# Buffers, addresses and order at the joints of a two-block transformer kernel: second buffers for normalized tiles and transposed matrices, raw weights in other places, loads and transposes in another order

## The chip, the cores and the metric

The kernel runs on one core of one Trainium2 chip. The metric is the device time of one execution in microseconds (us). The engines are TensorE (PE), VectorE (DVE), ScalarE (ACT), GpSimd (POOL) and SyncE (SP); SP issues nearly all the DMAs here, from one queue in order.

## What is computed

The input is 1024 tokens of width 1024 in fp32. A first block of two layers (attention of four kinds, gated projection, layer norm) gives x. The change concerns the second block:

```python
def swiglu(x, w_gate, w_up, w_down):
    return (jax.nn.silu(x @ w_gate) * (x @ w_up)) @ w_down
...
        h = h + 0.5 * swiglu(rms_norm(h, ffn1_norm[i]), ffn1_w_gate[i], ffn1_w_up[i], ffn1_w_down[i])
        u = rms_norm(h, mix_norm[i])
        z = u @ w_in[i]
        q, k, v, s_in, gates = jnp.split(z, splits, axis=-1)
...
        h = h + (g_attn * y_attn + g_ssm * y_ssm) @ w_out[i]
        h = h + 0.5 * swiglu(rms_norm(h, ffn2_norm[i]), ffn2_w_gate[i], ffn2_w_up[i], ffn2_w_down[i])
        h = h + (p[i] @ ple_w_proj[i]) * jax.nn.sigmoid(rms_norm(h, ple_norm[i]) @ ple_w_gate[i])
    return rms_norm(h, final_norm)
```

Between the two feed-forwards stand neighbourhood attention (y_attn) and a two-directional state-space branch (y_ssm), whose small matrices the kernel forms from the parameters. The feed-forward's hidden width is 2816.

## The kernel before

Every fp32 number that a product takes is split in two parts, hi and lo, and a product is three matmuls: hi by hi, lo by hi, hi by lo (`mm3`, L196 to L198). Splitting is done by ACT (the hi copy) and DVE or POOL (the lo difference); `operand` (L1009, L1010) does it for raw weights, into a ring of whi and wlo. Tokens are worked on as eight tiles of 128, four to a half. The order of instructions on each engine is set by a scheduler that takes the program's order as priority and a time model of its own; the chip runs each engine's list in that order. A new tile at the address of an older one waits for the older one's last use, so pool sizes and the order of allocation decide waits.

**Normalizing a tile.** `rms_tile` squares a tile on ACT (L945, into xn as scratch), takes the inverse root on DVE and POOL (L540, L541), and scales on DVE into xn (L947). PE transposes xn in eight 128x128 pieces, by `halves_in` (L960) ahead of a feed-forward and by `rms_T` (L258) behind one. xn has one buffer.

**Up phase** (`ffn_up`). A product of 2x2 blocks is formed from seven block products, which need sums of blocks of x (s1 to s4) and of the weights (t1 to t4). `halves_in` makes the x sums of tiles 4 to 7 with the single buffers a21, a11, s1, s2; `fourth` (L989, L998) makes the last one for four tiles. Raw weights come as `top` and `bot` [128, 4, 256] (L1061); POOL makes t1 to t4 of them (L1069 to L1072). These tiles lie in a late pool that opens over the tiles of `halves_in`. Eleven pairs of gate and up matrices follow; each finished hidden piece is stored at once (L1083).

**Down phase** (`ffn_down`). For each half of the tokens and each half of the columns there are 22 steps. A step loads a hidden piece (`hraw`, three buffers, L1128; only for the first column half), splits it (L1129, L1130), loads a weight piece (L1132; `draw` in even steps, `wraw` in odd ones, two buffers each) and does 12 matmuls. Beside the first half runs a generator `also`: in the first feed-forward it is `ssm_matrices`, which makes M and C on DVE (`cmul`, L1181 and L1184) for each of two directions, then 32 small products into Gp (L1273), then eight groups of two pairs of transposes (L1281), copied by ACT into gW (one buffer, L1283) and stored (L1285). C is stored in four large pieces (L1269). When a half is finished, `then` normalizes and transposes its tiles, the second half's with a priority put back by 150 (`later`).

```python
            for t in range(4):
                with self.later(hf * 150):
                    then(hf * 4 + t, h[t])
```

In the first block's last layer, the output tiles z (three buffers) go from the layer norm straight to a store (L1657) and to `rms_tile`.

## Time and profile before

| what | value |
|---|---|
| runs | 3683.14, 3685.1, 3699.77 us |
| median | 3685.1 us |
| profiled execution, its own time | 3689.25 us |
| its span, first to last instruction | 3687.4 us |
| PE busy | 3380.2 us (92%) |
| DVE, ACT, POOL busy | 2181.0, 1389.2, 1246.1 us |
| mean granted clock of PE | 0.955 |

The stages of the second block in the span: entry to the first up phase at about 1185 to 1256 us, its steady part to 1655, the first down phase to about 2032, the input products of the mix behind it; entry to the second up phase at 2826 to 2886, the second down phase from 3295 to 3542, and the last products to the end. PE is busy nearly all the time, so the time lost is the idle time of PE and the time in which its granted clock is at the lower of its two levels (1.2 instead of 2.4 GHz, shown as 0.50). Both are read by stretch.

### The profile page before, as it was taken

Reading aid. Unit: us, or ns where it says so; the run is one execution under the profiler, and the core shown is the slowest. Engines: PE = TensorE matmul, PEld = TensorE weight load, DVE = VectorE, ACT = ScalarE, POOL = GpSimd, SP = SyncE. Lnnn points to the kernel's source line nnn. Section 1 sums busy time; section 2 is a strip of 40 time slices with the busy share of each in tenths; the row PEclk is TensorE's granted clock in tenths of the full one; section 3 lists DMA queues with packets and bytes.
Section 4 is the critical chain, followed back from the end, with each engine's and each line's share of the span. In section 5 each row is a group of like instructions: output and inputs, shape, how many; then the busy total and the mean of one; then the engine's idle time right before and its main releaser. Section 6 shows DMA issues by size and latency. Waiting matters only on the chain. (4 is left out here: it accounts for less than half of the span.)

```text
span 3687.4 us, 53510 instructions
## 1 busy us (share of the span) xinstructions
PE 3380.2 (92%) x18872; PEld 2935.1 (80%) x18872; DVE 2181.0 (59%) x4926; ACT 1389.2 (38%) x3029; POOL 1246.1 (34%) x1082
## 2 busy tenths in 40 slices
PE   8999899999999599997869899798999799989988
PEld 7999798888888488876648688677789688878878
DVE  5656666656668766669241149435875866652235
ACT  3446645445646332323222131235632332333322
POOL 4232224333223633324314223162322533324522
PEclk9999999999999799997969899899999899999999
DMA  6667863567862222215443453467644322235433
GB/s 222 173 204 215 257 208 101 177 195 212 258 216 94 94 81 89 80 58 176 149 130 121 112 185 115 121 203 218 193 160 135 109 75 85 82 136 190 151 130 115
DMA packets 475355, 555.32 MB, mean 151 GB/s; under 512 B 45248, under 2 KB 318016, under 8 KB 475088
## 3 DMA queue, kind: packets, MB, share of 16 engines
q1 hardware_dynamic: 465872, 541.42, 47.4%
q10 hardware_dynamic: 9216, 10.49, 0.9%
q8 instruction: 150, 2.46, 0.3%
q14 instruction: 117, 0.96, 0.1%
HBM read 398.68 MB, written 153.06 MB: 150 GB/s over the span
## 5 line engine op out<-in xcount | busy, mean ns | idle before, releaser
L186 POOL TENSOR_SCALAR whi<-wraw 128x512 fp32r<-128x512 f32 (+1 forms) x288 | 185.6, 654 | 939.5 <-PE G L197 391.7
L196 PE MATMUL G<-xh,whi 128*128 128x512 f32 x1180 | 469.1, 398 | 3.4 <-DVE slo L161 2.6
L198 PE MATMUL G<-xh,wlo 128*128 128x512 f32 x1180 | 464.1, 394 | 0.0
L196 PE MATMUL G<-whi,xh 128*128 128x256 f32 (+2 forms) x1472 | 438.4, 298 | 27.7 <-ACT whi L1009 17.6
L197 PE MATMUL G<-wlo,xh 128*128 128x256 f32 (+2 forms) x1472 | 431.1, 293 | 0.0
L197 PE MATMUL G<-xl,whi 128*128 128x512 f32 x1064 | 420.4, 395 | 0.2 <-DVE xl L158 0.2
L196 PEld LDWEIGHTS G<-whi,xh 128*128 128x128 f32 x1472 | 282.5, 192 | 35.0 <-ACT whi L1009 18.5
L197 PEld LDWEIGHTS G<-wlo,xh 128*128 128x128 f32 x1472 | 282.4, 192 | 3.6
L188 POOL TENSOR_TENSOR wlo<-wraw,whi 128x512 fp32r<-128x512 f32 (+1 forms) x208 | 266.2, 1294 | 4.8
L196 PEld LDWEIGHTS G<-xh,whi 128*128 128x128 f32 x1180 | 223.7, 190 | 51.0 <-DVE slo L161 2.8
L198 PEld LDWEIGHTS G<-xh,wlo 128*128 128x128 f32 x1180 | 223.4, 189 | 45.7
L198 PE MATMUL G<-whi,xl 128*128 128x256 f32 (+2 forms) x832 | 249.6, 300 | 0.0
L198 PE MATMUL G<-whi,xh 128*128 128x256 f32 (+1 forms) x832 | 243.8, 294 | 0.6 <-DVE xh L1130 0.6
L197 PEld LDWEIGHTS G<-xl,whi 128*128 128x128 f32 x1064 | 201.9, 190 | 39.4 <-DVE xl L158 0.5
L1009 ACT ACTIVATE whi<-t 128x512 fp32r<-128x512 f32 x176 | 105.9, 624 | 320.2 <-PE G L197 147.1
L1010 POOL TENSOR_TENSOR wlo<-draw,whi 128x512 fp32r<-128x512 f32 x88 | 117.2, 1332 | 244.4 <-ACT whi L1009 241.4
L158 DVE TENSOR_TENSOR ptl<-T,pth 128x512 fp32r<-128x512 f32 (+2 forms) x296 | 181.7, 629 | 20.2 <-ACT pth L157 17.0
L502 PE MATMUL T<-ident,P 128*128 128x128 f32 x1064 | 185.4, 278 | 6.7 <-DVE P L481 5.7
L157 ACT ACTIVATE pth<-T 128x512 fp32r<-128x512 f32 (+2 forms) x296 | 156.3, 553 | 55.0 <-PE T L502 51.5
L509 PE MATMUL O<-pth,hv 128*128 128x256 f32 (+1 forms) x616 | 165.3, 280 | 9.4 <-ACT pth L157 3.1
L1071 POOL TENSOR_TENSOR t<-bot,top 128x512 f32<-128x512 f32 x44 | 65.6, 1492 | 316.6 <-DVE wlo L1010 314.9
L509 PE MATMUL O<-ptl,hv 128*128 128x256 f32 (+1 forms) x616 | 162.4, 295 | 5.4 <-DVE ptl L158 4.7
(570 smaller groups left out, 9200.2 us busy)
## 6 DMA issues: line engine op xcount, KB each, us to landing
wraw<-w_in SPq DMA_DIRECT2D x144, 256.0 KB, 3.3
wraw<-ffn_w_down SPq DMA_DIRECT2D x88, 256.0 KB, 3.0
hid<-r SPq DMA_DIRECT2D x88, 256.0 KB, 2.0
hraw<-hid SPq DMA_DIRECT2D x88, 256.0 KB, 3.7
draw<-ffn_w_down SPq DMA_DIRECT2D x88, 256.0 KB, 2.9
wraw<-w_out SPq DMA_DIRECT2D x64, 256.0 KB, 3.5
hk<-ka SPq DMA_DIRECT2D x48, 256.0 KB, 4.8
top<-ffn_w_gate SPq DMA_DIRECT2D x22, 512.0 KB, 3.7
```

What stands on the lines that cost most here:

```text
L157: nc.scalar.activation(hi, ps, AF.Copy)
L158: nc.vector.tensor_tensor(lo, ps, f(hi), op=OP.subtract)
L186: self.nc.gpsimd.tensor_scalar(hi, raw, 1.0, 0.0, op0=OP.mult, op1=OP.add)
L188: eng.tensor_tensor(lo, raw, f(hi), op=OP.subtract)
L196: t.matmul(out, lh, rh, start=first and i == 0, stop=False)
L197: t.matmul(out, lh, rl, start=False, stop=False)
L198: t.matmul(out, ll, rh, start=False, stop=last and i == n - 1)
L502: nc.tensor.transpose(ps[:, c + i * 128:c + i * 128 + 128], rows[bi][j], self.ident)
L509: nc.tensor.matmul(O[:, o:o + n], vs[j], p[:, c:c + n], start=nmm == 0, stop=not units and gi == len(grp) - 1 and x == 1, skip_group_check ...
L1009: self.nc.scalar.activation(as_src(hi), src, AF.Copy)
L1010: lo_eng.tensor_tensor(as_src(lo), src, as_src(f(hi)), op=OP.subtract)
L1071: nc.gpsimd.tensor_tensor(t3, b22, b12, op=OP.subtract)
```

## The change

The diff's core, in the order of the program:

```diff
 def rms_T, Next.done, second feed-forward's loop
-        x = self.T(p, [128, 1024], F32, "xn", 1)
+        x = self.T(p, [128, 1024], F32, "xn", 2)
 Next.tile
-                return K.T(p, [128, 1024], F32, "z", 3)
+                return K.T(p, [128, 1024], F32, "z", 2)
 def ffn_up
         p = late()
+        for n in ("t1", "t2", "t3", "t4"):
+            self.T(p, [128, 4, 128], F32, n, 1)
+        for n in ("th", "r3", "r4"):
+            tile(p, n, 2)
+        stores = []
+        def store():
+            for o, k, c in stores:
+                nc.sync.dma_start(hid[o:o + 128, k:k + 512], c)
+            stores.clear()
...
-                        o = j * 256 + n * 128
-                        nc.sync.dma_start(hid[o:o + 128, hf * 512:hf * 512 + 512], c)
+                        stores.append((j * 256 + n * 128, hf * 512, c))
                 done(c11, 0, 0)
+                if i == 0:
+                    store()
...
+        store()
 def ffn_down(..., delay=0)
                     if c == 0:
-                        raw = self.T(p, [128, 512], F32, "hraw", 3)
-                        nc.sync.dma_start(raw, hid[k * 128:k * 128 + 128, hf * 512:hf * 512 + 512])
-                        nc.scalar.activation(hi, raw, AF.Copy)
-                        nc.vector.tensor_tensor(lo, raw, f(hi), op=OP.subtract)
-                    raw = self.T(*((self.wp, [128, 512], F32, "wraw") if k % 2 else (p, [128, 512], F32, "draw")), 2)
+                        for i in range(3) if k == 0 else [k + 2] if k < 20 else []:
+                            raw = self.T(p, [128, 512], F32, "hraw", 3)
+                            nc.sync.dma_start(raw, hid[i * 128:i * 128 + 128, hf * 512:hf * 512 + 512])
+                            nc.scalar.activation(H[i][0], raw, AF.Copy)
+                            nc.vector.tensor_tensor(H[i][1], raw, f(H[i][0]), op=OP.subtract)
+                    raw = self.T(p, [128, 512], F32, "draw", 1) if k % 3 == 0 else self.T(self.wp, [128, 512], F32, "wraw", 2)
...
-                with self.later(hf * 150):
+                with self.later(hf * delay):
 calls of ffn_down: delay 60 in the first feed-forward, 400 in the second
 def ssm_matrices
+            def group(gp):
                 ps = self.PS("O", self.nO)
-                W = self.T(p, [128, 2, 2, 2, 64], F32, "gW", 1)
+                W = self.T(p, [128, 2, 2, 2, 64], F32, "gW", 2)
...
             for k in range(1, 9):
                 self.cmul(C[...])
-                if k % 2 == 0:
-                    yield
+                yield
+                if k == 2:
+                    (the 32 products into Gp, and Gs)
+                elif k > 2:
+                    group((k - 3) * 2)
             (the four stores of C)
-            (the 32 products into Gp, and Gs; the eight groups, a yield after every second)
+            for gp in (12, 14):
+                yield
+                group(gp)
 second feed-forward's set-up
         p = self.pool("xn2", 1)
+        g = self.rms_gain(p, I["ffn2_norm_2"])
+        for n in ("a21", "a11", "s1", "s2"):
+            self.T(p, [128, 4, 128], F32, n, 1)
+        for _ in range(2):
+            self.T(p, [128, 1024], F32, "xn", 2)
         h.append(p.tile([128, 4, 1024], F32, name="h1"))
-        g = self.rms_gain(p, I["ffn2_norm_2"])
```

In words: normalized tiles get two buffers and z two instead of three. In the late pool t1 to t4 and the small result tiles come first, so `top` and `bot` lie at other addresses: `top` over the layer norm's gains and `bot` over z, where they had lain over the norm's gain rg and over a21 and a11. The program lists the hidden stores one matrix later. The down phase lists its hidden loads up to three steps ahead and has three raw weight buffers instead of four. The second half's normalizing has its priority put back by 60 or 400 instead of 150. In `ssm_matrices` the small products and the transposes' groups are listed between the steps of C, and gW has two buffers. Lines behind about L1050 move by 10 to 22.

Three places show what the engines' lists make of this. On ACT, at the entry to the first up phase (T_16313 and T_16398 are the transposes of tiles 5 and 6; a their first copies; the xn of z_16380 and z_16465 belong to tiles 6 and 7), the list was before

```order
L975 ACTIVATE a_3833_16323<-T_16313 128x512
L945 ACTIVATE xn_16391,rms_16392<-z_16380 128x1024
L157 ACTIVATE xh_3806_16217<-T_16318 128x4x128
L157 ACTIVATE xl_3807_16218<-s_3835_16325 128x4x128
L157 ACTIVATE sb_16219<-s_3836_16333 128x4x128
L157 ACTIVATE sc_16220<-a_3833_16323 128x4x128
L975 ACTIVATE a_3851_16408<-T_16398 128x512
L945 ACTIVATE xn_16474,rms_16475<-z_16465 128x1024
```

and is now

```order
L157 ACTIVATE sc_16220<-a_3815_16238 128x4x128
L1009 ACTIVATE whi_16428<-wraw_16447 128x512
L945 ACTIVATE xn_16391,rms_16392<-z_16380 128x1024
L1038 ACTIVATE r_3837_16340<-G_16347 128x512
L975 ACTIVATE a_3833_16323<-T_16313 128x512
L945 ACTIVATE xn_16474,rms_16475<-z_16465 128x1024
L157 ACTIVATE xh_3806_16217<-T_16318 128x4x128
```

The squares of tiles 6 and 7 have each moved one tile forward: tile 7's stand behind the copy of tile 5, not of tile 6.

On PE, at the end of the first half's products of the first down phase (eh, el the last hidden pieces; gen, xl the second direction's parameters and matrices), the list was before

```order
L198 MATMUL S_20467<-whi_21033,el_19620 128x512
L1281 MATMUL O_20418<-ident,xl_4472_19884 128x128 x2
L1281 MATMUL O_20427<-ident,xl_4472_19884 128x128 x4
L1273 MATMUL O_20839<-gen_19831,xl_4556_20527 128x32 x32
L1281 MATMUL O_20873<-ident,xl_4556_20527 128x128 x4
```

and is now

```order
L198 MATMUL S_20443<-whi_20979,el_19627 128x512
L1282 MATMUL O_20552<-ident,xl_4481_19899 128x128 x4
L1295 MATMUL O_20806<-gen_19846,xl_4568_20584 128x32 x32
L1282 MATMUL O_20881<-ident,xl_4568_20584 128x128 x4
L1282 MATMUL O_20912<-ident,xl_4568_20584 128x128 x4
```

One pair of the first direction's transposes less stands behind the products (a row of four is a group of two pairs); the second direction's 32 small products and all its eight groups still stand behind them.

On PE, in the input products behind the first down phase (T the transposes of xn; G the products), the list was before

```order
L198 MATMUL G_22276<-xh_4616_21098,wlo_22189 128x512
L258 MATMUL T_22091<-ident,xn_22084 128x128 x4
L258 MATMUL T_22098<-ident,xn_22084 128x128 x4
L258 MATMUL T_22112<-ident,xn_22105 128x128 x4
L258 MATMUL T_22119<-ident,xn_22105 128x128 x4
L258 MATMUL T_22133<-ident,xn_22126 128x128 x4
L258 MATMUL T_22140<-ident,xn_22126 128x128 x4
L196 MATMUL G_22302<-xh_4765_22061,whi_22158 128x512
```

and is now, for the last tile,

```order
L198 MATMUL G_22283<-xh_4623_21105,wlo_22196 128x512
L258 MATMUL T_22140<-ident,xn_22133 128x128 x4
L258 MATMUL T_22147<-ident,xn_22133 128x128 x4
L196 MATMUL G_22309<-xh_4772_22068,whi_22165 128x512
```

The transposes of tiles 5 to 7 stood together behind the first half's products; now only tile 7's do, and those of tiles 4, 5 and 6 stand among the products, with 24, 24 and 17 matmuls to the next.

## Rows read from the trace of the kernel before

**Rows 1.** Windows: busy us (instructions) of PE, PEld, DVE, ACT, POOL; PEclk; DMA share; GB/s.

```profile
1200.00:1250.00 50.00, 15.25 (x71) 12.30 (x69) 35.19 (x40) 17.39 (x30) 29.75 (x23) 0.65 0.10 32
...
1350.00:1400.00 50.00, 50.00 (x223) 41.39 (x222) 33.78 (x48) 15.80 (x28) 14.18 (x10) 1.00 0.31 95
...
1850.00:1900.00 50.00, 23.66 (x92) 17.16 (x91) 18.21 (x46) 7.28 (x19) 0.00 (x0) 0.50 0.29 84
...
2050.00:2100.00 50.00, 41.99 (x180) 34.50 (x179) 9.33 (x16) 9.97 (x19) 16.70 (x19) 0.86 0.27 85
...
3550.00:3600.00 50.00, 37.29 (x282) 35.98 (x280) 25.40 (x46) 16.58 (x46) 8.56 (x13) 0.83 0.41 149
```

**Rows 2.** Timeline of PE, 1216 to 1256: start, length, line, [idle before <-releaser].

```profile
1216.40 1.94 PE L960 MATMUL T<-ident,xn 128*128 128x128 f32 x8 [5.03 <-DVE xn L947]
...
1225.27 1.94 PE L960 MATMUL T<-ident,xn 128*128 128x128 f32 x8 [6.93 <-DVE xn L947]
...
1255.39 0.80 PE L196 MATMUL S<-sb,whi 128*128 128x512 f32 x1 [28.18 <-ACT whi L1009]
```

**Rows 3.** Timeline of ACT, tile 6's and tile 7's first copies, tile 6's last.

```profile
1217.52 0.60 ACT L975 ACTIVATE a<-T 128x512 f32<-128x512 f32 x1 [3.96 <-PE T L960]
...
1221.81 0.63 ACT L157 ACTIVATE sc<-a 128x512 fp32r<-128x512 f32 x1 [0.59 <-POOL a L983]
...
1226.39 0.60 ACT L975 ACTIVATE a<-T 128x512 f32<-128x512 f32 x1 [3.96 <-PE T L960]
```

**Rows 4.** Timelines of POOL (three rows) and DVE (two), the same entry.

```profile
1220.51 1.27 POOL L983 TENSOR_TENSOR a<-a,a 128x512 f32<-128x512 f32 x1
...
1222.70 1.34 POOL L989 TENSOR_TENSOR a<-xh,sa 128x512 f32<-128x512 f32 x1
...
1253.41 1.26 POOL L1070 TENSOR_TENSOR t<-bot,t 128x512 f32<-128x512 f32 x1 [5.89 <-DMA bot<-ffn_w_gate]
...
1191.95 1.28 DVE L947 SCALAR_TENSOR_TENSOR xn<-z,rrs,rg 128x1024 f32<-128x1024 f32 x1
...
1222.85 2.28 DVE L947 SCALAR_TENSOR_TENSOR xn<-z,rrs,rg 128x1024 f32<-128x1024 f32 x1
```

**Rows 5.** Timeline of PE, state-space matrices of the second direction, 1829 to 1901.

```profile
1829.38 0.52 PE L1281 MATMUL O<-ident,xl 128*128 128x128 f32 x2 [2.63 <-ACT gW L1283]
...
1848.07 0.61 PE L1273 MATMUL O<-gen,xl 128*128 128x32 f32 x2 [18.17 <-DVE xl L1181]
...
1863.35 0.69 PE L1281 MATMUL O<-ident,xl 128*128 128x128 f32 x2 [0.69 <-ACT gen L1275]
...
1883.75 0.69 PE L1281 MATMUL O<-ident,xl 128*128 128x128 f32 x2 [8.63 <-ACT gW L1283]
...
1888.55 0.69 PE L1281 MATMUL O<-ident,xl 128*128 128x128 f32 x2 [0.47 <-ACT gW L1283]
...
1891.07 0.69 PE L1281 MATMUL O<-ident,xl 128*128 128x128 f32 x2 [1.83 <-ACT gW L1283]
...
1900.03 0.80 PE L196 MATMUL G<-whi,xl 128*128 128x512 f32 x1 [0.99 <-ACT xl L1129]
```

**Rows 6.** Timeline of PE, transposes of finished tiles (L258).

```profile
1929.39 1.94 PE L258 MATMUL T<-ident,xn 128*128 128x128 f32 x8 [3.01 <-DVE xn L947]
...
2059.86 1.94 PE L258 MATMUL T<-ident,xn 128*128 128x128 f32 x8 [4.06 <-DVE xn L947]
...
3554.56 1.73 PE L258 MATMUL T<-ident,xn 128*128 128x128 f32 x7 [4.00 <-DVE xn L947]
```

**Rows 7.** Timeline of PE, entry to the second up phase.

```profile
2867.16 1.97 PE L960 MATMUL T<-ident,xn 128*128 128x128 f32 x8 [6.46 <-DVE xn L947]
```

**Rows 8.** Timeline of PE, first direction's small products (L1273).

```profile
1731.54 0.63 PE L1273 MATMUL O<-gen,xl 128*128 128x32 f32 x2 [11.64 <-DVE xl L1181]
```

**Rows 9.** The page's DMA issues (KB each, median us to landing); timeline of SP.

```profile
draw<-ffn_w_down SPq DMA_DIRECT2D x88, 256.0 KB, 2.9
...
3289.84 0.90 SPq L1128 DMA_DIRECT2D hraw<-hid  x2
```

More of the change, by code (lines that the diff above doesn't have):

```diff
@@ L1104, in four, with ffn_down @@
         return [(W[0][:, k * 128:k * 128 + 128], W[1][:, k * 128:k * 128 + 128]) for k in range(4)]
-    def ffn_down(self, hid, wd, src, dst, p, slots, then, also=None):
+    def ffn_down(self, hid, wd, src, dst, p, slots, then, also=None, delay=0):
         nc = self.nc
@@ L1285, in ssm_matrices @@
                 nc.sync.dma_start(self.win_d[:, b0:b0 + 4, :], W.rearrange("p q e x s -> p (q e) (x s)"))
-                if gp % 4 == 2:
-                    yield
+            for k in range(1, 9):
+                src = (cc[:, 0], cc[:, 1]) if k == 1 else (C[:, 0, :, cs_(k - 1)], C[:, 1, :, cs_(k - 1)])
+                self.cmul(C[:, 0, :, cs_(k)], C[:, 1, :, cs_(k)], src[0], src[1], bc16(lbr), bc16(lbi), u1, u2, conj=True)
+                yield
+                if k == 2:
+                    Gp = self.PS("O", self.nO)
+                    for gp in range(16):
+                        for x in range(2):
+                            nc.tensor.matmul(Gp[:, gp * 32:gp * 32 + 32], M[:, x, gp].rearrange("p j i -> p (j i)"),
+                                             cb[:, x, gp].rearrange("p e o -> p (e o)"), start=x == 0, stop=x == 1)
+                    nc.scalar.activation(Gs[d], Gp.rearrange("p (g e o) -> p g e o", g=16, e=2), AF.Copy)
+                elif k > 2:
+                    group((k - 3) * 2)
+            for x in range(2):
+                for e in range(2):
+                    nc.sync.dma_start(self.wout_d[x * 64:x * 64 + 64, bs, e], C[e * 64:e * 64 + 64, x].rearrange("p g j o -> p g (j o)"))
+            for gp in (12, 14):
+                yield
+                group(gp)
         yield
-        z = self.T(p, [128, 2, 2, 2, 64], F32, "gW", 1).rearrange("p a b c d -> p (a b c d)")
+        z = self.T(p, [128, 2, 2, 2, 64], F32, "gW", 2).rearrange("p a b c d -> p (a b c d)")
         v.memset(z[96:128], 0.0)
@@ L1662, in done @@
                              s2=two(slot(self.sx, "sb")), s3=two(slot(self.sx, "sc")))
-                x = K.T(self.p, [128, 1024], F32, "xn", 1)
+                x = K.T(self.p, [128, 1024], F32, "xn", 2)
                 K.rms_tile(z, x, self.g)
@@ L1705, in then @@
             self.rms_T(h, *rms, xM, t)
-        self.ffn_down(nx.hid, I["ffn1_w_down_2"], nx.hd, hd, p, places(nx.sx, ("xh0", "xl0"), ("xl1", "xh1"), ("sa", "sb", "sc"), 1), then, also())
+        self.ffn_down(nx.hid, I["ffn1_w_down_2"], nx.hd, hd, p, places(nx.sx, ("xh0", "xl0"), ("xl1", "xh1"), ("sa", "sb", "sc"), 1), then, also(), 60)
         self.lo_dve = False
@@ L1769, in second_block @@
         h3 = dr([1024, 1024], "h3d")
-        self.ffn_down(hid, I["ffn2_w_down_2"], h2, h3, p, places(sx, ("xh0", "xh1"), ("xl0", "xl1"), ("sa", "sc", "sb")), then, also())
+        self.ffn_down(hid, I["ffn2_w_down_2"], h2, h3, p, places(sx, ("xh0", "xh1"), ("xl0", "xl1"), ("sa", "sc", "sb")), then, also(), 400)
         self.close(p, sx)
```

15 lines of the change are left out of this document (1 added, 14 removed).

## The prediction, made before the changed kernel ran

> **What bounds the kernel now.** I began with the busy time per stretch [rows 1]. In steady stretches, 1350 to 1400 us for one, TensorE (PE) is busy for all 50 us at the full granted clock (1.00), with 223 matmuls, 0.224 us each, so nothing that the change does there can shorten them. Idle PE time lies in a few joints between phases, where the same rows show both a low busy time and a granted clock between its two levels: 15.25 of 50 us after 1200 (clock 0.65), 23.66 after 1850 (0.50, the lower level all through), 41.99 after 2050, 37.29 after 3550. The change is therefore worth what it does to the waits in those joints. I read them next in the timeline of PE, where the last column says how long it stood idle before a group and what ended that.
>
> Into the first feed-forward up phase [rows 2] it waits 5.03 and 6.93 us for normalized tiles 6 and 7 (xn) and 28.18 us for the first operand of the new weights. In the state-space matrices [rows 5] it waits 18.17 us for VectorE (DVE), then again and again for single copies into gW. At the ends of token halves [rows 6] it waits for xn, and before the second up phase [rows 7] again for xn. Steps before about 1150 us keep their places on PE and gain nothing.
>
> **The change, part by part.** No instruction is added or removed; order, buffers and addresses change.
>
> *Entry to the first up phase.* xn has one buffer: the squares of tile 7 may not start before tile 6 is transposed, so tiles follow each other at 8.87 us (1217.52 to 1226.39 [rows 3]). With two, xn of tile 7 is made while tile 6 is put away. In the new order of ScalarE (ACT) it stands ahead of tile 6's copy, where it stood behind it. What then sets the pace is the single a21, s1, s2: copy at 1217.52, last ACT piece from 1221.81 to 1222.44, then a DVE operation of some 0.7: about 6 us. So the 5.03 before tile 6 go (tile 6 is ready while PE still has early products), tile 7 comes 2.9 sooner (8.87 less 6), and the fourth operands behind it move up with it. Next POOL waits 5.89 us for the weights' lower half (bot) [rows 4], whose buffer lay where a11 and a21 are used to the end; now it lies over z, whose last reader is xn of tile 7, so the load lands under the fourth operands and those 5.9 go too. Sum 5.0 + 2.9 + 5.9 = 13.8; I take **-14**. z gets two buffers for three: a tile must be stored and normalized before the next but one begins. PE's early products cover this; if it costs one tile's pace at the old rate I lose 6, and if the early products end in no wait at all I win 3 more: -5 to -17.
>
> *Stores one matrix later.* On the queue of SyncE (SP) the hidden stores stand row for row between the same loads as before. Cost and gain: 0.
>
> *Loads of the down phase.* SP issues three hraw loads, then the first weight load, so that load leaves about 0.9 us later (two issues of 0.45 [rows 9]). In the first down phase this is covered: PE stands at the first state-space products until DVE has its matrices, 11.64 us [rows 8], and DVE's work up to there is the same. So an earlier hidden half cures small gaps and hands the time to that wait: 0, within 3 either way. In the second nothing covers it: **+1**.
>
> *State-space matrices, second direction.* The order now spreads two more pairs of the first direction's transposes among products, but all 16 pairs of the second still come after the products, behind its 32 small products. Two things get shorter. The first direction's last pairs wait for gW, 2.63 us the last time; with two gW buffers, and one pair less behind the products, they don't, so DVE's matrices start, and PE's 18.17 us wait ends, some 3.5 us sooner. Then the pairs: a group of two takes 0.69 + 0.47 + 0.69 + 1.83 = 3.68 us, the last wait because gW is single and the next copy needs a store's landing. With two, a group can take 2 x (0.69 + 0.47) = 2.3, 8 groups 19 against 36.7 us (1863.35 to 1900.03, with one wait of 8.63 behind the four large stores of C). The large stores stay on the same queue and hold one small store, so I leave 6 us of their hold: 25 against 36.7. Together 3.5 + 11.7 = 15; I take **-14**. Bounds: -6 if the large stores hold all the small ones, -20 if none.
>
> *Transposes at the ends of halves.* At 2059.86 and 2065.76 PE waits 4.06 and 3.95 us (one of the two rows stands) and then runs the eight transposes in 1.94 us at the lower clock. In the new order the four tiles' groups are spread over the input products, with 24 products, 5.4 us, between two (17 before the last). Today a whole tile, chain and transposes, takes 4.06 + 1.94 = 6.0 us, and with two buffers its chain runs under the tile before. Cover is thus enough; the gaps (8.0), half of 1.94 twice (1.9) and about 1 us of slow products behind go: **-11** (-6 if POOL, which makes the inverse root, is held by weight splits of 1.3). The 3.01 at 1929.39 goes likewise: **-3**. Near the end, at 3554.56, there are three such gaps of about 4.0 (one row stands); here nothing stands between the groups, so tile 5 comes at once, while tile 6 waits about 3 and tile 7 about 1.5 for their chain: 11.9 + 2.9 of slow transposes, less 4.5: **-10** (-5 to -13).
>
> *Entry to the second up phase.* Of the 6.46 us before tile 7 some 5 go, as above; what stands behind it stays, since a21, a11 and the sums keep one buffer: **-5** (0 to -8).
>
> **Sum:** -14 + 1 - 14 - 11 - 3 - 10 - 5 = -56. The profiled execution took 3689.25 us (span 3687.4), 4 above the median of three runs, 3685.1: 3633 for it, **3629** for the median. A difference under 0.5%, 18 us, I count as no change that a measurement can tell.
>
> **A rule against it.** Beside POOL, DVE's xn takes 2.28 us instead of 1.28, and began 0.15 us after a POOL operation of 1.34 [rows 4]: it stood still for about as long as POOL worked. I take such losses as already in the pace of 6. The Trainium skill (SBUF — State Buffer, Terms) says that the two engines' shared port pair is held exclusively for a whole instruction, the loser blocking fully. By that rule moving xn ahead doesn't make it free; the row's 1.0 agrees. As a mechanism it is the second rival, priced from rows.
>
> **The rivals.**
>
> 1. *Half comes through.* The single buffers left (a21, a11, s1, s2), the large stores on SP's queue and the inverse roots on POOL become the next waits. For it: the 8.63 wait [rows 5] in the transposes is the queue's, not gW's, and every joint has such a chain. Against: in each joint the wait that goes is the longest at its place. Half of 56 is 28: **3657**.
>
> 2. *DVE and POOL take turns.* POOL's work per tile is 3.9 us in three operations (1.34, two of 1.27) and up to one more for the inverse root, DVE's 3.2 (xn 1.28, three splits of half the width): 8.1 if nothing overlaps, nearly the 8.87 of today. Then tiles don't get closer in either entry: the sum loses 8 and 5, **3642**. Against it: tile 7's xn is made early, under products.
>
> 3. *The weights' buffers run out: slower.* The down phases had four raw buffers for w_down (two draw, two wraw) and now have three, draw a single one. A buffer comes back every third step, 3 x 12 x 0.224 = 8.1 us, where it was 10.8. In that time fit an issue (0.45), the load, ACT's split (0.63 [rows 3]), POOL's (about 1.3) and, estimated, 0.5 of hand-overs: the load may take 5.3 us. Median is 2.9 [rows 9]; each us above the point costs up to one in each of 59 rounds (176 steps, every third). Slower than before overall from a typical load of 5.3 + 75/59, about 6.6 us; a load of 7 us would give 3629 + 100 = **3729**. Against it: loads would have to be over twice as slow as the median.
>
> 4. *It doesn't do what it says.* The stores stay where they were on SP, the second direction's transposes stay behind the products. If the other moves too are undone by waits: **3685**.
>
> **How the numbers follow.** Forecast (3612 to 3645) 0.58; rival 1 (3645 to 3666) 0.20; rival 2 (3642) 0.08; the bounds' far side, under 3612, 0.04; rival 4, 0.05; rival 3, 0.05. Faster by over 0.5% (below 3667): 0.90, same 0.05, slower 0.05. The range that holds eight in ten takes the forecast, rival 2, most of rival 1 and part of the far side: 3606 to 3660.
>
> **What would show it.** Right, step by step: the second group of transposes after 1200 us about 6 us behind the first and no POOL wait for bot; the pairs after the second direction's small products in 22 to 28 us with gaps behind gW only around the large stores; no gap over 1 us before the transposes of the input products; gaps of at most 3 in the last joint. Wrong: waits for draw or hraw inside the down phases (rival 3), tiles still 8 to 9 us apart at both entries (rival 2), or the same sums of idle with other names (rivals 1 and 4). If PE's wait at the first direction's small products moves by more than 3 us, DVE's work there was not the same and my zero is wrong.

## The result, and the profile after

The changed kernel takes **3648.7 us** (median of four runs, 3643.66 to 3653.89) against 3684.1 for the kernel before on the same chip (3681.3 to 3699.77): the medians are 35.4 us apart, and the ratio of the runs is 0.9895, 95% interval 0.9864 to 0.9926. Run once more at the end, beside new runs of the kernel before, it took 3639.3 against 3680.9: 41.5 less, ratio 0.9884 (0.9866 to 0.9903). Both lie inside the range (3606 to 3660), with 35 to 42 us of the 56 forecast. Of the bands in it, the second median lies in the forecast's own (3612 to 3645), the first in that of rival 1 (3645 to 3666), by which half comes through.

The windows of the changed kernel at the joints, columns as in [rows 1]; each is moved about as far as its joint moved (10, 15, 30 and 40 us; the steady one stays):

```profile
1190.00:1240.00 50.00, 18.45 (x84) 13.60 (x82) 39.39 (x43) 19.86 (x35) 34.59 (x23) 0.71 0.27 84
1350.00:1400.00 50.00, 50.00 (x222) 41.44 (x221) 33.35 (x48) 15.22 (x27) 18.52 (x12) 1.00 0.22 69
1835.00:1885.00 50.00, 32.74 (x118) 24.52 (x119) 26.12 (x62) 11.86 (x26) 0.37 (x1) 0.52 0.40 113
2020.00:2070.00 50.00, 49.70 (x232) 41.09 (x231) 7.66 (x13) 9.57 (x17) 17.60 (x19) 1.00 0.43 101
3510.00:3560.00 50.00, 44.74 (x350) 43.34 (x349) 25.90 (x49) 16.39 (x47) 8.45 (x14) 0.93 0.47 164
```

The steady part is as full as before. The joints behind the input products (fourth row) and at the end (fifth) have filled up, and their granted clock rose from 0.86 to 1.00 and from 0.83 to 0.93. The first is still two thirds empty.

To see where the time went I divided the profiled executions at the same PE instructions. Work ahead of the change differs from run to run by some 5 us, so the first stretch starts at the end of the attention's last product of queries and keys (L448) in front of the entry. "After" and "again" are the two profiles of the changed kernel.

| stretch, to the first product or transpose of the next | before | after | again | moved | forecast |
|---|---|---|---|---|---|
| last query-key product, to first up phase | 123.8 | 115.0 | 114.9 | -8.8 | -14 |
| first up phase, to the down phase's first product | 406.9 | 411.8 | 412.3 | +5.0 | 0 |
| first down phase, to state-space products | 69.3 | 64.4 | 63.3 | -4.9 | 0 |
| those, to the second direction's | 116.5 | 116.0 | 117.6 | -0.5 | -3.5 |
| second direction, to the product behind the pairs | 52.0 | 41.4 | 41.4 | -10.6 | -10.5 |
| to the scan of the state-space branch | 216.5 | 203.4 | 203.1 | -13.1 | -14 |
| to the second up phase (over the attention, which alone differs by some 5 us from run to run) | 765.9 | 763.4 | 759.2 | -2.5 | -5 |
| second up phase, to the down phase's first product | 412.9 | 412.6 | 412.0 | -0.3 | +1 |
| second down phase, to the last projection | 293.9 | 286.8 | 286.2 | -7.1 | -10 |

The sum of the moves is -43; the two profiled executions, 3689.25 and 3643.66, are 45.6 apart, the rest being 3 us ahead of the first mark. (The medians are closer together because the execution profiled before was 5 us above its median and the one after the fastest of its four.)

### The profile page after: what moved, and what is told of

It is laid out like the page before. It is cut to its first block, busy times and chain, and to the rows that moved or that the text cites. A ratio compares the mean times of both kernels' runs of the same rounds, so it can differ in the third digit from the quotient of the medians.

```text
span 3641.9 us, 53515 instructions
## 1 busy us (share of the span) xinstructions
PE 3370.9 (93%) x18872; PEld 2925.8 (80%) x18872; DVE 2178.9 (60%) x4926; ACT 1391.4 (38%) x3029; POOL 1254.8 (34%) x1082
## 5 line engine op out<-in xcount | busy, mean ns | idle before, releaser
L196 PEld LDWEIGHTS G<-whi,xh 128*128 128x128 f32 x1472 | 281.0, 191 | 36.2 <-ACT whi L1009 20.1
L1010 POOL TENSOR_TENSOR wlo<-wraw,whi 128x512 fp32r<-128x512 f32 x112 | 152.7, 1370 | 182.3 <-ACT whi L1009 178.3
```

Source lines behind the costliest of these rows:

```text
L196: t.matmul(out, lh, rh, start=first and i == 0, stop=False)
L1010: lo_eng.tensor_tensor(as_src(lo), src, as_src(f(hi)), op=OP.subtract)
```

## What the rows of the changed kernel show

Entry to the first up phase, PE, to be read beside [rows 2]:

```profile
1214.38 1.12 PE L960 MATMUL T<-ident,xn 128*128 128x128 f32 x4 [5.98 <-ACT a L975]
...
1243.67 0.79 PE L196 MATMUL S<-sb,whi 128*128 128x512 f32 x1 [26.03 <-ACT whi L1009]
...
1247.51 0.80 PE L198 MATMUL S<-sb,wlo 128*128 128x512 f32 x1 [2.62 <-DVE wlo L1010]
```

ACT, the first copies of tiles 5, 6 and 7 ([rows 3]); then DVE, and POOL beside xn and at bot ([rows 4]):

```profile
1203.95 0.60 ACT L975 ACTIVATE a<-T 128x512 f32<-128x512 f32 x1 [3.65 <-DVE sc L158]
...
1213.73 0.60 ACT L975 ACTIVATE a<-T 128x512 f32<-128x512 f32 x1 [3.30 <-DVE sc L158]
...
1220.45 0.60 ACT L975 ACTIVATE a<-T 128x512 f32<-128x512 f32 x1 [1.65 <-DVE sc L158]
...
1210.76 2.28 DVE L947 SCALAR_TENSOR_TENSOR xn<-z,rrs,rg 128x1024 f32<-128x1024 f32 x1 [0.44 <-POOL rrs L541]
1212.96 0.68 DVE L158 TENSOR_TENSOR sc<-a,sc 128x512 fp32r<-128x512 f32 x1
...
1243.42 1.76 DVE L1088 SCALAR_TENSOR_TENSOR r<-th,r 128x512 f32<-128x512 f32 x1
...
1210.70 1.25 POOL L989 TENSOR_TENSOR a<-xh,sa 128x512 f32<-128x512 f32 x1
...
1241.36 1.59 POOL L1080 TENSOR_TENSOR t<-bot,t 128x512 f32<-128x512 f32 x1
```

PE waits for xn no more; the wait is now for ACT's copy, which needs the buffer a back, and that hangs on DVE's last split of the tile before (sc). Tile 7's copy is 6.72 us behind tile 6's, as forecast (about 6), and POOL no longer waits for bot. But tile 6's copy is 9.78 behind tile 5's (8.60 before): xn of tile 7 (2.28 us) stands on DVE ahead of that last split.

Part of the gain is paid back at once. The wait of 2.62 us behind the first product, for the lo part of a weight from DVE, is new. In the 44.6 us from the first product on, the granted clock is 0.91 where it was 0.95, and they hold 173 products instead of 187. At 0.224 us a product [rows 1] that is some 3 of the 8.8 us. With the longer wait at the next joint (9.09 us for the first w_down instead of 7.33) it makes the +5.0 in the second row of the table.

State-space matrices, second direction: PE ([rows 5]), one DVE row with the POOL row beside it, then SP's queue:

```profile
1835.89 0.61 PE L1295 MATMUL O<-gen,xl 128*128 128x32 f32 x2 [19.27 <-DVE xl L1195]
...
1865.56 0.69 PE L1282 MATMUL O<-ident,xl 128*128 128x128 f32 x2 [3.95 <-ACT gW L1284]
1870.88 0.69 PE L1282 MATMUL O<-ident,xl 128*128 128x128 f32 x2 [3.47 <-ACT gW L1284]
1877.30 0.80 PE L196 MATMUL G<-whi,xl 128*128 128x512 f32 x1 [0.99 <-ACT xl L1143]
...
1816.66 1.52 DVE L1195 TENSOR_TENSOR xl<-gu,gu 128x256 f32<-128x256 f32 x1 [1.31 <-PE O L1282]
1816.65 1.26 POOL L1010 TENSOR_TENSOR wlo<-wraw,whi 128x512 fp32r<-128x512 f32 x1
...
1857.15 1.34 SPq L1302 DMA_DIRECT2D ssm_wout<-xh  x2
1858.59 1.94 SPq L1286 DMA_DIRECT2D ssm_win<-gW  x1
1860.62 2.92 SPq L1302 DMA_DIRECT2D ssm_wout<-xh  x2
```

From the first transposes (1851.17) to the product behind them it takes 26.1 us, forecast 25, and two waits are left, near the large stores. DVE's matrices start only 1.6 us sooner after the first direction's products (96.8 us instead of 98.4), and their first operation takes 1.52 us where its neighbours take 0.42.

Transposes of finished tiles ([rows 6]), the second entry ([rows 7]: PE's first product, ACT's copies of tiles 4 to 7), the second down phase in its middle, and the first direction's small products ([rows 8]):

```profile
1908.00 1.26 PE L258 MATMUL T<-ident,xn 128*128 128x128 f32 x8 [2.26 <-DVE xl L158]
1916.16 1.25 PE L258 MATMUL T<-ident,xn 128*128 128x128 f32 x8 [1.42 <-DVE xl L158]
...
3518.11 1.94 PE L258 MATMUL T<-ident,xn 128*128 128x128 f32 x8 [2.64 <-DVE xn L947]
3520.72 1.09 PE L258 MATMUL T<-ident,xn 128*128 128x128 f32 x4 [0.67 <-DVE xn L947]
...
2844.10 0.79 PE L196 MATMUL T<-sa,whi 128*128 128x512 f32 x1 [19.09 <-ACT whi L1009]
...
2804.65 0.60 ACT L975 ACTIVATE a<-T 128x512 f32<-128x512 f32 x1
2813.24 0.60 ACT L975 ACTIVATE a<-T 128x512 f32<-128x512 f32 x1 [3.33 <-DVE xl L158]
2823.70 0.60 ACT L975 ACTIVATE a<-T 128x512 f32<-128x512 f32 x1 [1.13 <-DVE xl L158]
2832.21 0.60 ACT L975 ACTIVATE a<-T 128x512 f32<-128x512 f32 x1 [1.65 <-DVE xl L158]
...
3377.79 0.63 ACT L1009 ACTIVATE whi<-wraw 128x512 fp32r<-128x512 f32 x1 [2.06 <-DMA wraw<-ffn_w_down]
...
3378.98 2.57 DVE L1144 TENSOR_TENSOR sb<-hraw,sb 128x512 fp32r<-128x512 f32 x3 [5.09 <-ACT sb L1143]
3381.47 0.68 DVE L1161 SCALAR_TENSOR_TENSOR ht<-G,ht 128x512 f32<-128x512 f32 x1
...
3382.29 0.47 PE L196 MATMUL G<-whi,xl 128*128 128x512 f32 x1 [2.15 <-DVE ht L1161]
...
1719.89 0.64 PE L1295 MATMUL O<-gen,xl 128*128 128x32 f32 x2 [11.53 <-DVE xl L1195]
```

The gaps behind the input products are gone and the last joint has 3.3 us left of three times 4.0. And there is a **new wait** that no term of my sum had: ACT waits for a w_down block (2.06), three hidden splits follow on ACT and DVE, the drain (DVE's reading of the finished sums, which frees them for the next products) stands behind them, and PE waits 2.15. The load of that block took 2.7 us, less than the median of 3.0, so it is its issue that came late.

At the second entry, to be read beside the 19.09 above, the kernel before had

```profile
2882.42 0.79 PE L196 MATMUL T<-sa,whi 128*128 128x512 f32 x1 [13.30 <-ACT whi L1009]
```

So the 6.46 us for xn of tile 7 [rows 7] went, and the wait behind it grew by 5.8. PE's waits of 0.3 us and more in the 90 us ahead of that product sum to 21.6 us before and 20.1 now. The copies of tiles 4 to 7 span 27.6 us instead of 30.4, 8.5 to 10.5 apart where they were 8.9 to 11.2.

In the first down phase, ahead of the small products, the kernel before had waits for hidden pieces, the longest

```profile
1698.56 0.79 PE L198 MATMUL G<-whi,sb 128*128 128x512 f32 x1 [4.27 <-DVE sb L1130]
```

These are gone; four of 0.5 to 1.2 us for POOL's splits of weights stand in their place.

## The experiments

Each is the changed kernel with one edit. "First entry" and so on are the stretches of the table. The changed kernel's own two medians, on two chips, are 9.4 us apart (3648.7, 3639.3), so what an edit of some us is worth is read from the stretches.

**One gW buffer.**

```diff
- W = self.T(p, [128, 2, 2, 2, 64], F32, "gW", 2)
+ W = self.T(p, [128, 2, 2, 2, 64], F32, "gW", 1)
```

> The changed kernel with one gW buffer instead of two, all else kept. Theory (each joint gains by its own part): the second buffer alone made the pairs of transposes behind the second direction's small products shorter, 26.1 us in the changed kernel (1851.2 to 1877.3) against 36.7 before; with one buffer they take 35 to 38 again, the run is 9 to 12 us longer than the changed kernel (3656 to 3661), and nothing else moves by over 2 us. Rival (the store queue is the limit, not the buffer): the pairs stay within 3 us of 26.

3659.75 us, ratio to before 0.9926 (0.9908 to 0.9944). The second direction takes 51.5 us (41.4; before 52.0), with the old waits of 1.8 and one of 8.2:

```profile
1877.12 0.69 PE L1282 MATMUL O<-ident,xl 128*128 128x128 f32 x2 [8.18 <-ACT gW L1284]
1880.77 0.69 PE L1282 MATMUL O<-ident,xl 128*128 128x128 f32 x2 [1.80 <-ACT gW L1284]
```

The same count stands once more behind the pairs and is changed with it. The second buffer is worth 10.1 us: shown.

**One xn buffer in the first entry, the rest as changed.**

```diff
- x = K.T(self.p, [128, 1024], F32, "xn", 2)
+ x = K.T(self.p, [128, 1024], F32, "xn", 1)
```

> The changed kernel with one xn buffer at the first entry (z keeps two). Theory (the second buffer lets tile 7 follow tile 6 by 6.7 us instead of 8.9 and takes the 5.0 us wait before tile 6): the first product of the up phase is 4 to 8 us later, the run 4 to 8 longer. Rival (DVE and POOL take turns, so the pace per tile is theirs whatever the buffers): within 2 us.

3655.88 us, ratio 0.9913 (0.9891 to 0.9935). First entry 121.9 us (115.0; before 123.8): the second xn is worth 6.8 there, and PE waits 6.83 and 6.92 for xn again. POOL does not wait for bot, and tile 6's copy comes some 3.5 us later after the common mark than in the kernel before, which also had one xn but three z. So having two z may cost something here; no run shows it by itself.

**One xn buffer behind the feed-forwards.**

```diff
- x = self.T(p, [128, 1024], F32, "xn", 2)
+ x = self.T(p, [128, 1024], F32, "xn", 1)
```

> The changed kernel with one xn buffer for the transposes of finished tiles, delays kept at 60 and 400. Theory (the gaps before these transposes went because of the second buffer): the waits of about 4 us come back, two behind the first down phase and two or three behind the second; 8 to 12 us more in the first place and 5 to 8 in the second, the run 12 to 20 longer. Rival (the changed priority alone spread them): under 5 longer.

3668.22 us, ratio 0.9961 (0.9943 to 0.9979), 19.5 above the changed kernel. The stretch to the scan takes 213.6 us (203.4), and the last joint, from the first transposes of the second down phase to the end, 9.1 more, with its three gaps again:

```profile
3541.67 1.72 PE L258 MATMUL T<-ident,xn 128*128 128x128 f32 x8 [4.01 <-DVE xn L947]
3547.34 1.94 PE L258 MATMUL T<-ident,xn 128*128 128x128 f32 x8 [3.95 <-DVE xn L947]
3553.23 1.94 PE L258 MATMUL T<-ident,xn 128*128 128x128 f32 x8 [3.95 <-DVE xn L947]
```

Another 6.5 us stand in the middle of the second down phase. There the other variants lose 1 to 6.5 us with two xn; this is told of below and is not the work of xn.

**Up-phase buffers allocated late, as before.**

```diff
-        for n in ("t1", "t2", "t3", "t4"):
-            self.T(p, [128, 4, 128], F32, n, 1)
-        for n in ("th", "r3", "r4"):
-            tile(p, n, 2)
```

> The changed kernel without the early allocation of t1 to t4, th, r3, r4, so that top and bot lie at the start of the late pool again. Theory: the wait of POOL for bot comes back in the first entry (about 5.9 us), but the 2.6 us that PE waits behind its first two products there, for DVE working beside POOL, shrinks; the first product of the up phase is 4 to 7 us later and the steady part starts 2 to 5 later; the run is 2 to 6 longer. Rival (the addresses gave all 11.7 us of the first entry): 10 to 12 longer. Second rival (fourth operands bind anyway): within 1.

3651.69 us, ratio 0.9903 (0.9877 to 0.993). My expectation for the first entry missed: 115.3 us, no wait for bot. The wait of 5.89 is thus gone for another reason than this allocation (the other buffer counts move the addresses too; that was not taken apart). In the second entry PE's wait grows from 19.09 (the same to 0.01 us in nearly all other variants) to 23.24, but the up phase behind it takes 409.0 us instead of 412.6: of the 4 us all but 0.5 come back, and the early allocation is not shown to earn anything.

**Stores at once.**

```diff
- stores.append((j * 256 + n * 128, hf * 512, c))
+ o = j * 256 + n * 128
+ nc.sync.dma_start(hid[o:o + 128, hf * 512:hf * 512 + 512], c)
```

> The changed kernel with the stores of an output matrix's partial sums issued at once, as before, instead of one matrix later. My term: 0. SP runs ahead of the first users of what it brings, so a store that stands behind the next matrix's loads or ahead of them hides either way: down phases within 2 us of the changed kernel's (from the first product of the first down phase to the state-space's first small products 64.4 us there; from the second down phase's first product to the PLE stage's first product 286.8 us). Rival: the stores that wait for POOL's or DVE's sums hold the loads behind them on SP, and the loads of the down phase three steps ahead only help together with the later stores: then new waits for the raw weights of the down phase of 2 us and more each, 10 us and more in all.

3650.14 us, ratio 0.9906 (0.989 to 0.9922); down phase to the state-space products 63.5 us (64.4). The stores' term of 0 stands. The second down phase took 292.4 (286.8), for a wait told of below.

**Hidden blocks one step at a time.**

```diff
- for i in range(3) if k == 0 else [k + 2] if k < 20 else []:
+ for i in [k]:
```

> The changed kernel with the half of the hidden products that the down phase reads loaded one row block at its own step again, instead of three at the first step and then one two steps ahead. My theory: in the first joint between an up and a down phase the first product of the down phase waits 9.1 us in the changed kernel against 7.3 before, because three loads stand ahead of the first w_down on SP; with one load a step it goes back to 7 to 8, and what is won there is lost again at the state-space's first small products (wait for DVE's matrices, 11.5 us there, grows by as much), so the time to that mark stays within 1.5 us. Rival: the loads ahead do spare waits inside the down phase; then products of the down phase show waits for the hidden products' raw blocks of 1 us and more each, and from the down phase to the mark it takes 5 us longer, in the second down phase 5 to 10 us.

3650.69 us, ratio 0.9907 (0.989 to 0.9924). The first product of the down phase waits 7.50 us (9.09), and the state-space products come 1.5 us sooner (474.7 from the first up product, against 476.2), so the 1.6 won are not paid at their wait (11.04). They are paid behind it, and more: the second direction's products come 596.6 us after the first up product, against 592.2 and 593.2 in the two profiles of the changed kernel. Between the two, a w_down block stands on SP behind four stores of wout (5.60 us of issue), ACT waits 9.52 for it, and PE behind ACT:

```profile
1761.53 0.69 PE L1282 MATMUL O<-ident,xl 128*128 128x128 f32 x2 [4.57 <-ACT gW L1284]
```

Whether the loads ahead spare this wait, or only the new order on SP makes it, is open. In the stretch ahead of the small products they change nothing (63.8 us against 64.4), and in the second down phase the waits told of below stay (138.6 us to the first transposes).

**Stores of wout behind the last pairs.**

```diff
-            for x in range(2):
-                for e in range(2):
-                    nc.sync.dma_start(self.wout_d[x * 64:x * 64 + 64, bs, e], ...
             for gp in (12, 14):
                 yield
                 group(gp)
+            for x in range(2):
+                for e in range(2):
+                    nc.sync.dma_start(self.wout_d[x * 64:x * 64 + 64, bs, e], ...
```

> The changed kernel with the four stores of the second matrix of the state-space pairs (wout) moved behind the last two groups of pairs, so that on SP the last windows' loads no longer stand behind them. Theory: the two waits left among the pairs of the second direction (3.95 and 3.47 us for the loads of a window that stand behind these stores on SP) go or fall under 1 us each: from the second direction's small products to the first product behind the pairs about 35 us instead of 41.4, and the whole 5 to 7 us less. Rival A: the loads themselves (their bytes beside the stores of the queue's other entries) set the time: gaps stay within 2 us of what they are. Rival B: the stores then delay the loads of the next stage, and the joint of the state-space's input products grows by what the pairs lose: total within 2 us of the changed kernel.

3649.98 us, ratio 0.9904 (0.9887 to 0.9922), 41.5 us for the second direction; but SP issued wout in the old places, so this tested nothing. The same stores **on ACT's queue**:

```diff
- nc.sync.dma_start(self.wout_d[x * 64:x * 64 + 64, bs, e], ...
+ (nc.scalar if d else nc.sync).dma_start(self.wout_d[x * 64:x * 64 + 64, bs, e], ...
```

> The changed kernel with the second direction's four stores of wout issued by ACT on its own queue instead of by SP; the run that was to move them on SP left SP's order as it was, so that the question stayed open. Theory: the waits of 3.95 and 3.47 us among the second direction's pairs are the time in which the windows' stores stand behind the wout stores on SP. With these on ACT each of the two waits goes below 1.5 us; ACT spends some 0.7 us of issue on each of four stores between its copies, so that from the second direction's small products to the first product behind the pairs it takes 36 to 39 us instead of 41.4 to 41.7. Rival: the bytes of wout (64 rows of 16 pieces each) hold the DMA engines, whichever queue asks for them: then the windows' stores land as late as before and the stretch stays within 1.5 us of 41.5.

3652.05 us, ratio 0.9906 (0.988 to 0.9931); the stretch takes 41.0. ACT, its copies and its queue (ACTq):

```profile
1860.78 2.35 ACTq L1302 DMA_DIRECT2D ssm_wout<-xh  x2
1863.54 0.38 ACT L1284 ACTIVATE gW<-O 128x256 f32<-128x256 f32 x1 [2.38 <-issue]
1863.55 2.10 ACTq L1302 DMA_DIRECT2D ssm_wout<-xh  x1
1865.69 0.38 ACT L1284 ACTIVATE gW<-O 128x256 f32<-128x256 f32 x1 [1.78 <-issue]
...
1872.73 0.38 ACT L1284 ACTIVATE gW<-O 128x256 f32<-128x256 f32 x1 [4.08 <-DMA ssm_win<-gW]
```

The last two of the four issues cost 1.7 and 2.1 us, not my 0.7, and delay ACT's own copies; a store of a window still lands late (4.08). The stretch stays within 1.5 us of 41.5, which is the rival's number. Its reason, the bytes, is not shown by that, since ACT now waits behind the issues as well: PE's waits (2.08, 1.47, 3.78) sum to 7.3 us, where two summed to 7.4. Whether wout's bytes or its issue sets them is open.

**The fourth sums in buffers of their own.**

```diff
- a12 = self.T(p, [128, 4, 128], F32, "a11", 1)
+ odd = s2 is None and sl.start // 128 % 2
+ a12 = self.T(p, [128, 4, 128], F32, "a12" if s2 is not None else "a21" if odd else "a11", 1)
...
- s2 = self.T(p, [128, 4, 128], F32, "s2", 1)
+ s2 = self.T(p, [128, 4, 128], F32, "s1" if odd else "s2", 1)
```

> The changed kernel with buffers of their own for the fourth sum of each tile: in the first entry two tiles' sums alternate between two pairs of buffers, in the second entry this sum has a buffer that no other sum uses. Theory: the four last steps of the first entry take 4 us each because POOL and DVE pass one buffer back and forth (1.26 sum, 0.81 and 0.63 waits, 1.26 sum); with two pairs POOL's next sums run while DVE subtracts and splits: 2.6 to 3.2 us a step, the first up product 3 to 5 us sooner. In the second entry the tiles come 8.5 to 10.5 us apart with POOL idle 2.6 us of each turn, waiting for DVE's split before the fourth's sum; with its own buffer that sum stands ahead and the pace falls to 6.5 to 7.5 us a tile, PE's wait of 19.1 us there to 12 to 15. Rival: both engines run slower beside each other (sums of 1.26 to 1.7 us, splits of 0.7 to 1.5), so that the pace is the sum of their work whatever the buffers: both waits within 1.5 us of what they are.

3643.11 us, ratio 0.9885 (0.9863 to 0.9906). First entry 112.8 us (-2.3). In the second PE's wait falls to 14.82, with a new one of 2.37 behind it:

```profile
2827.28 0.80 PE L196 MATMUL T<-sa,whi 128*128 128x512 f32 x1 [14.82 <-ACT whi L1010]
...
2831.72 0.80 PE L198 MATMUL T<-sa,wlo 128*128 128x512 f32 x1 [2.37 <-DVE wlo L1011]
```

The copies of tiles 4 to 7 span 27.3 us there (2791.17 to 2818.47; changed kernel 27.6): the pace did not fall, only the sum behind the last tile came sooner. On the pace the rival's forecast came true, not its reason: in the changed kernel's 27.6 us DVE is busy 22.25 and POOL 18.29, so they do overlap, and a21, a11, s1 and s2 stay single. The two entries gain 2.3 and 3.7 us, but the second down phase needs 139.6 us to its first transposes (133.2), by the waits told of next. Its median is the lowest of these variants, but its interval overlaps the changed kernel's, so it is not shown to be faster.

**Four raw buffers again in the second down phase.** In the middle of this phase the variants wait longer than the changed kernel, for the input pin (a block of the last projection's input p) and at the drain. In the kernel with one xn behind the feed-forwards:

```profile
3349.35 0.41 PE L1598 MATMUL S<-ident,pin 128*128 128x128 f32 x2 [2.42 <-DMA pin<-p]
...
3404.59 0.47 PE L196 MATMUL G<-whi,xl 128*128 128x512 f32 x1 [2.62 <-DVE ht L1161]
```

So there were to be four raw buffers again. First paid for with one of the three hraw buffers:

```diff
- for i in range(3) if k == 0 else [k + 2] if k < 20 else []:
-     raw = self.T(p, [128, 512], F32, "hraw", 3)
+ a = 2 if delay == 400 else 3
+ for i in range(a) if k == 0 else [k + a - 1] if k < 23 - a else []:
+     raw = self.T(p, [128, 512], F32, "hraw", a)
...
- raw = self.T(p, [128, 512], F32, "draw", 1) if k % 3 == 0 else self.T(self.wp, [128, 512], F32, "wraw", 2)
+ n = 2 if delay == 400 else 1
+ raw = self.T(p, [128, 512], F32, "draw", n) if k % (4 - n) == 0 else self.T(self.wp, [128, 512], F32, "wraw", 2)
```

> The changed kernel with two raw buffers of the down phase's own again in the second down phase, so that w_down turns over four raw buffers there, as before, instead of three; paid for with one of the three buffers for the hidden products' raw blocks in that phase (two loaded ahead instead of three). Theory, formed from the trace of the changed kernel and six of its variants: the change gave back 5 to 8 us in the middle of the second down phase, which no term of my sum had. There ACT waits 2.06 us for a w_down block that is loaded late, the hidden products' splits stand behind it on ACT and DVE, the drain of the four sums behind those, and PE waits 2.15 us for the drain (2.0 to 2.9 in the variants); in eight of the nine variants PE also waits 0.9 to 2.4 us for the load of the transposed input pin, and some 10 to 13 matmuls behind these waits run at 0.43 us apart instead of 0.23. With four raw buffers both waits go below 0.5 us, and from the second down phase's first product to the first transposes of its first half's outputs it takes 131 to 133 us (131.3 before, 133.2 in the changed kernel's profile, 136.1 to 139.7 in seven variants); the whole 4 to 8 us below the changed kernel's 3648.7. Rival: the waits come from the loads' place on SP (behind the stores of the first half's outputs), whatever the buffers: then 2 us and more for the drain stay, and 136 us and more to that mark.

3653.88 us, ratio 0.9911 (0.9884 to 0.9939). The two waits are gone, but a larger one stands ahead of them, behind hidden blocks that came late:

```profile
3329.65 0.77 PE L196 MATMUL G<-whi,xh 128*128 128x512 f32 x1 [11.65 <-DVE ht L1163]
```

So the payment hid the effect. Paid for with the second xn of that phase instead (hraw as changed, the draw lines as above):

```diff
- def rms_T(self, h, p, g, xT, t, tag="T"):
+ def rms_T(self, h, p, g, xT, t, tag="T", n=2):
...
- x = self.T(p, [128, 1024], F32, "xn", 2)
+ x = self.T(p, [128, 1024], F32, "xn", n)
...
- self.rms_T(h, rp, g, xP, t)
+ self.rms_T(h, rp, g, xP, t, n=1)
```

> The changed kernel with two raw buffers of the down phase's own in the second down phase (four for w_down in all, as before), this time paid for with the second buffer for the normalised tile in that phase; the blocks of hidden products keep their three buffers. The run before that paid with one of these got rid of the two new waits in the middle of the phase, but the drain between the two column halves of the first half then waited 11.65 us, behind splits of hidden blocks that arrived late. Theory: the new waits come from three raw buffers instead of four. With four, no wait for the transposed input pin (2.4 us), for the drain between the halves below 0.5 us (2.0 to 3.1 with three), and no 11.65: from the phase's first product to the first transposes of its outputs 130 to 133 us, against 133.2 to 139.7 with three. The end of the phase has the waits of about 4 us each before its transposes back (10 us as in the run with one such buffer), so that the whole is at 3655 to 3668. Rival: the three-step loads of hidden blocks, which this kernel keeps, crowd SP and cause the waits: then they stay at 2 us and more, and 136 us and more to that mark.

3644.67 us, ratio 0.9895 (0.9874 to 0.9916). PE has no wait over 0.6 us from the phase's first product to the last joint; the first transposes come 131.0 us into the phase (before 131.3, changed 133.2, with one xn and three raw buffers 139.7). Three raw buffers instead of four are the cause of the new waits: shown, as far as edits can that also move addresses. The three kernels with four (before, and these two) have neither of these two waits, all eleven profiles with three have the one at the drain (1.9 to 3.1 us), and loading hidden blocks one at a time did not cure it. It has the last joint's gaps (4.01, 3.95, 3.95) and is not told apart from the changed kernel (3639.3 beside it on the same chip, the intervals overlapping).

**The changed kernel once more.**

> The changed kernel itself, once more. Expected if its profile was a lucky one in the second down phase: median 3646 to 3652, and in its profile the wait for the input pin of 0.9 to 2.4 us and the wait for the drain of 2 to 3 us, with the first transposes 136 us and more after the phase's first product (133.2 in the profile shown). Rival: the variants' edits caused these waits, and this profile repeats 133 us with one wait of about 2.1.

3639.34 us, ratio 0.9884 (0.9866 to 0.9903). I missed: it repeats 132.8 us and a wait of 2.05, none for the input pin. All nine variants that keep three raw buffers do wait for pin (0.9 to 2.4 us) and need 134 to 140 us. So its first profile was no lucky one. Why the changed kernel itself is spared the wait for pin is something that these runs don't show.

## Why the prediction was right, and by how much not

- **Direction and places: right in the main.** Every joint that was to gain gained, but two hardly (the second direction's start and the second entry). Undoing a second buffer gives back, at its own place, 10.1 us for gW, 6.8 for xn in the first entry, and 10.2 and 9.1 for xn behind the feed-forwards. Not taken apart are the second xn of the second entry, the two z, and the new priorities (60 and 400 for 150).
- **Pairs of the second direction (11.7 forecast, 10.6): right**, with the remaining waits around the large stores. Their earlier start was mis-sized: 0.5 instead of 3.5, and 1.1 later in the second profile. PE's last first-direction wait is still 1.34 us, and DVE's first operation takes 1.52 instead of 0.42 because it starts beside a POOL split (1.26 us from 1816.65).
- **Transposes at the ends of halves (-11, -3): right**, -13.1, but the sign of no gap over 1 us failed: waits of 2.26 and 1.42 for DVE are new. The variants that keep this second xn take 199.0 to 204.6 us here, so the 13 is known to some 3 us. The last joint (-10) gave about 9.
- **Entry to the first up phase (-14): the step that failed most**, -8.8, and some 3 of these were paid back behind the first product. I counted PE's 5.03 before tile 6 as won. Against the common mark tile 6's copy came 0.8 us sooner, not 5; tile 7's distance won another 2.1 and bot 5.8. Putting xn of tile 7 ahead on DVE delays the end of tile 5, and a has one buffer. A wait of PE's that goes is worth only what the next engine in the chain can use. The wait for bot went, as forecast. That bot's new place over z is the reason is not shown, since the wait is also gone with the old order of allocation.
- **Entry to the second up phase (-5): failed**, about -1. Rival 2's sign is what appeared: copies 8.5 to 10.5 us apart, and still 27.3 us for three with another buffer. That the engines take turns is not shown, since their busy times overlap; what the rows show is that each of the last three copies waits for DVE's last split of the tile before (3.33, 1.13, 1.65), which reads the single buffer.
- **Loads of the down phase (0 and +1): the 0 came out by luck.** The forecast let an earlier hidden half cure small gaps and hand the time to the wait at the small products, DVE's work up to there being the same. The gaps went, but the wait stayed (11.53 against the 11.64 of [rows 8]; 8.06 in the second profile, a move of the kind that was to show the zero wrong), and the products came 4.9 us sooner after the first w_down product: DVE was busy 63.5 of 64.4 us there, where it had been 66.1 of 69.3. Which edit did this is open; with hidden blocks loaded one at a time it is the same. The 5.0 us lost ahead of it, in the entry and at the first w_down, made the sum zero. The +1 sat in the wrong place: the second joint itself did not grow, but the middle of the phase did, by 1.9 in the changed kernel and by more in most variants. Rival 3 named the cause, three raw buffers. I had priced it for a steady stretch with a median load and so found room (5.3, by its own terms 5.2, against 2.9); where the halves meet, three hidden splits stand between, and the margin is gone.
- **Stores one matrix later: 0, right.**

On the rule against it: DVE's xn of tile 7 took 2.28 us, beginning 0.06 us behind a POOL sum of 1.25. The three long DVE rows above (2.28, 1.76, 1.52) are each longer than their like by 1.0 to 1.1 us. The Trainium skill (SBUF — State Buffer, Terms) says that the port pair the two share is held for a whole instruction while the loser waits. These rows agree.

By the table the terms fell short by 5.2 us (first entry), 3.0 (earlier start), 0.9 (transposes), 2.5 (second entry, with the attention ahead of it) and 2.9 (second down phase), while the second joint did 1.3 better than its +1. That is 13 of the 56, and leaves the 43 of the traces. What is missing went mostly as rival 1 has it: at both entries the single buffers left became the next wait.

## What to carry to other kernels

A second buffer pays where one engine's copy waits for a transfer (gW: 10 us) or where a chain can run under other work (xn behind the feed-forwards: 10.2 and 9.1); where two engines pass one tile back and forth it moved most of the wait to the next single buffer. Count what pays for a buffer: here one of four raw weight buffers paid, and the price came up not in the steady loop but at the seam of two halves. Check the order on the queue after an edit meant to move a transfer: one run here moved nothing. And look at the parts of a stretch that moved by 0: here it held +5.0 and -4.9.

## What was not expected of the hardware

Two things. A DVE operation of 0.42 us took 1.52 beside one POOL operation of 1.26. In the three rows above the loss is 1.0 to 1.1 us whether the operation alone takes 0.42, 0.69 or 1.28, so that for its length the shortest suffers most. And issuing a store of 64 rows of 16 pieces from ACT took up to 2.1 us, in which ACT's copies behind it stood still, while the pairs of such stores had taken 1.34 and 2.92 us of SP's queue.
